# Transposing the eleventh feed-forward chunk with the DMA crossbar instead of TensorE

## The chip, the cores and the metric

The kernel runs on one core of a Trainium2 chip. The metric is the device time of one execution in microseconds (us). An execution is compared through the median of several runs.

## The reference, cut to what matters

Four decoder layers work on one sequence of 256 tokens with 1024 features. A layer is a token mixer (differential attention in layers 0 and 3, stick-breaking attention in layer 1, sliding-window attention in layer 2) and a SwiGLU feed-forward with a hidden width of 2816. Both sit between two RMS norms.

```python
x = x + rms_norm(mixer(rms_norm(x, g0)), g1)
f = (silu(h @ w_gate) * (h @ w_up)) @ w_down      # h = rms_norm(x, g2)
x = x + rms_norm(f, g3)
```

Everything is float32. All weights are read once; only the feed-forward is touched by the change.

## The kernel before, in words

**Two streams.** The 256 tokens are two streams of 128 rows (`stream(0)`, `stream(1)`, line 924). Both use every weight tile while it is in SBUF, the first stream ahead of the second.

**Units.** The weights come in units of 128 x 1024 float32 (512 KB). SP loads a unit into one of four `stage` buffers (`load_dma`, line 242), ACT makes the rounded high part `hi` and DVE the rest `lo` (`split`, line 254), both in a ring of eleven. A product of two float32 matrices is three TensorE products of rounded parts: high x high, low x high and high x low. One unit is six products of 512 columns for a stream.

**Feed-forward** (`ffn`, line 871). The hidden width is cut into eleven chunks of 256 (NCH = 11, c = 0 to 10). A chunk is projected by four units into one PSUM bank (`project`, line 496); ACT and DVE make t and then `h`, 128 rows by 256 hidden columns. For the down projection `h` has to be transposed, two blocks of 128 x 128, and split into `hTh` and `hTl`. `down(c)` (line 880) waits for the event `(name, "h", c)`, takes two units and adds twelve products to `acc`. The calls follow the list `downs` (line 214): behind chunk c from 1 to 8 comes `down(c - 1)`, behind chunk 9 none, behind chunk 10 `down(8)`, `down(9)` and `down(10)`.

**Two ways to transpose.** Chunks 0 to 9 go through `turn` (line 891): GpSimd copies `h` into two planes of 16-bit halves, SP issues one transposing DMA (both in `by_dma`, line 561), GpSimd puts the halves together again (`words`, line 569), ACT and DVE split (`split_rows`, line 576). Chunk 10 is transposed on TensorE behind `down(9)` (lines 914 to 919), into the PSUM bank `th`, and split from there.

**The order of the work.** `Emitter` (line 42) writes the instructions of both streams and of spawned tasks in one order. It keeps a time of its own that grows with the products it emits, a unit by 6 x 512 / 2.4 ns = 1.28 us and a transpose by 0.21 us. A generator yields `("d", ns)` to pause for that time, `("e", key)` to wait for an event and `("w",)` to take the next unit. Tasks that are due come first, then the first stream, but the second stream wherever it has yet to pass an edge (the end of a mixer's input projection, or of a layer) that the first has reached:

```python
behind = any(self.pos[1] < w <= self.pos[0] for w in self.edges)
order = mains[::-1] if behind else mains
```

The first stream may be at most LAG = 8 units ahead. Splits are emitted up to AHEAD = 3 units ahead of it and eleven ahead of the second, loads STAGE = 4 units ahead of the splits. Past the start of the first layer the calls `act`, `dve`, `pool` and `pe` (class `Start`, line 172) do not hold the emitted order any more: the framework then orders each engine's instructions by what its own model of the program takes to be ready, and prefers the one emitted first.

**Layer ends.** After `down(10)` a stream runs `post_norm` (line 457), pauses for 4.0 us, and with a layer to follow runs `pre_norm` (line 418): eight transposes of x into `tp_n` on TensorE, `xh_n` in eight pieces on ACT, `xl_n` on DVE. Then it pauses 0.6 us and projects the next mixer's first chunk. In layers 1 and 3 that chunk takes four units. In layer 2 it takes two, and a pause of 2.0 us follows. When the first stream is through with a layer, the second still has the last units of chunk 10 and then the units of chunks 8, 9 and 10 ahead of it.

Of the kernel before, what the change touches and what calls it, by code (L numbers as in the profile page):

```python
# [9 lines left out]
F32 = mybir.dt.float32  # L10
F32R = mybir.dt.float32r
# [8 lines left out]
P = 128  # L20
# [5 lines left out]
NCH = HIDDEN // 256  # L26
# [8 lines left out]
TMP = 8  # L35
# [123 lines left out]
def trunk_kernel(ctx, tc, x, positions, norm_gains, a_w_in, a_w_out, a_lambda, a_subln, b_w_in, b_w_out,  # L159
                 c_w_in, c_w_out, c_sinks, w_gate, w_up, w_down, out, depth=DEPTH):  # L160
# [4 lines left out]
    wk = ctx.enter_context(tc.tile_pool(name="wk", bufs=2))  # L165
# [3 lines left out]
    def bank(tag, s, shape, name):  # L169
        return ps.tile(shape, F32, tag=f"{tag}{s}", name=name, bufs=BANKS[tag])  # L170
# [43 lines left out]
    def downs(c):  # L214

        return range(c - 1, c) if 0 < c < NCH - 2 else range(NCH - 3, NCH) if c == NCH - 1 else ()
# [45 lines left out]
    em = Emitter(load_dma, split, len(units), edges)  # L262
# [123 lines left out]
    def transpose(o, i):  # L386
        pe.transpose(o, i, ident)
        em.t += P * COLUMN_NS * 4
# [81 lines left out]
    def rows_product(acc, ah, al, w, first, last):  # L470

        cols = [slice(h * 512, (h + 1) * 512) for h in range(2)]
        if last:
            for h, cs in enumerate(cols):
                mm3(acc[h], ah, al, w[0][:, cs], w[1][:, cs], first, last)
        else:
            for v in range(2):
                for h, cs in enumerate(cols):
                    mm(acc[h], ah, w[v][:, cs], first and v == 0, False)
            for h, cs in enumerate(cols):  # L480
                mm(acc[h], al, w[0][:, cs], False, False)
# [14 lines left out]
    def project(s, xn, n, units_, name, first, tag="mm"):  # L496

        b = bank("acc" if first else tag, s, [P, n], f"mm_{name}")
        per = KT // units_
        for u in range(units_):  # L500
            w = yield ("w",)
            js = [(per * u + j, slice(j * n, (j + 1) * n)) for j in range(per)]
            for kt, cs in js:
                for v in range(2):
                    mm(b, xn[0][:, kt, :], w[v][:, cs], kt == 0 and v == 0, False)
            for kt, cs in js:
                mm(b, xn[1][:, kt, :], w[0][:, cs], False, kt == KT - 1)
        return b
# [52 lines left out]
    def by_dma(src, n, name):  # L561

        planes = wk.tile([P, 2, n * P], U16, tag="t2k", name=f"hp_{name}", bufs=TMP)
        pool.tensor_copy(planes, src.bitcast(U16).rearrange("p (n w) -> p w n", w=2))
        turned = wk.tile([P, 2, n, P], U16, tag="t2k", name=f"hq_{name}", bufs=TMP)
        nc.sync.dma_start_transpose(turned.rearrange("p w b t -> p (w b) t"), planes.rearrange("p w n -> p (w n)"))
        return turned

    def words(dst, turned):

        pool.tensor_copy(dst.bitcast(U16).rearrange("p b (t w) -> p w b t", w=2), turned)
# [4 lines left out]
    def split_rows(oT, sl, src, scale=None):  # L576

        hi, lo = oT[0][:, sl, :], oT[1][:, sl, :]
        if scale is None:
            act.activation(hi, src, AF.Copy)  # L580
            dve.tensor_tensor(lo, src, hi.bitcast(F32), ALU.subtract)
        else:
            act.activation(hi, src, AF.Copy, scale=scale)
            dve.scalar_tensor_tensor(lo, src, scale, hi.bitcast(F32), ALU.mult, ALU.subtract)
# [286 lines left out]
    def ffn(s, i, xn):  # L871
        name = f"f{i}{s}"
        half = sm.tile([P, 1], F32, tag=f"half{s}", name=f"half_{name}", bufs=1)
        hsq = sm.tile([P, 1], F32, tag=f"hsq{s}", name=f"hsq_{name}", bufs=1)
        dve.tensor_scalar(half, xn[2], 0.5, None, ALU.mult)
        dve.tensor_tensor(hsq, half, xn[2], ALU.mult)
        acc = None
        hT = {}

        def down(c):  # L880
            nonlocal acc
            yield ("e", (name, "h", c))
            for j in range(2):
                w = yield ("w",)
                if acc is None:
                    acc = [bank("acc", s, [P, 512], f"acc_{name}_{q}") for q in range(2)]
                j2 = 2 * (c % 2) + j
                rows_product(acc, hT[c][0][:, j2, :], hT[c][1][:, j2, :], w, c == 0 and j == 0, c == NCH - 1 and j == 1)
            del hT[c]

        def turn(c, h):
            yield ("d", 2600)
            turned = by_dma(h, 2, f"{name}{c}")
            yield ("d", 4200)
            if c % 2 == 0:
                hT[c] = hT[c + 1] = [wk.tile([P, 4, P], F32R, tag=f"o{q}{s}", name=f"hT{q}_{name}{c}") for q in "hl"]
            t = wk.tile([P, 2, P], F32, tag="t2k", name=f"hx_{name}{c}", bufs=TMP)
            words(t, turned)
            split_rows(hT[c], slice(2 * (c % 2), 2 * (c % 2) + 2), t)
            em.set((name, "h", c))  # L900

        for c in range(NCH):
            chunk = yield from project(s, xn, 512, 4, f"{name}{c}", c == 0, ("tp", "mm")[c % 2])
            t = wk.tile([P, 256], F32, tag=f"as{s}", name=f"t_{name}{c}", bufs=STEPS)
            h = wk.tile([P, 256], F32, tag=f"as{s}", name=f"h_{name}{c}", bufs=STEPS)
            act.activation(t, chunk[:, 0:256], AF.Tanh, scale=half)
            dve.scalar_tensor_tensor(t, t, 1.0, chunk[:, 0:256], ALU.add, ALU.mult)
            dve.scalar_tensor_tensor(h, t, hsq, chunk[:, 256:512], ALU.mult, ALU.mult)
            if c < NCH - 1:
                em.spawn(turn(c, h))  # L910
            for d in downs(c):
                if d < NCH - 1:
                    yield from down(d)
        tp = bank("mm", s, [P, 2, P], f"th_{name}")
        for j in range(2):
            transpose(tp[:, j, :], h[:, j * P:(j + 1) * P])
        hT[c] = [wk.tile([P, 4, P], F32R, tag=f"o{q}{s}", name=f"hT{q}_{name}{c}") for q in "hl"]
        split_rows(hT[c], slice(2 * (c % 2), 2 * (c % 2) + 2), tp)
        em.set((name, "h", c))
        yield ("d", 700)  # L920
        yield from down(NCH - 1)
        return acc

    def stream(s):
        if s:
            yield ("d", 1500)
        for i in range(depth):
            kind = i % 3
            xn = pre_norm(s, 4 * i, f"n{i}{s}")
            yield ("d", 600)  # L930
            if i == 0 and s:
                scalars()
                act.on = dve.on = pool.on = pe.on = False
            gain = gain_of(i, 1)
            oT, name = yield from (layer_a, layer_b, layer_c)[kind](s, i, xn)
            acc = yield from out_proj(s, oT, name, (1, 1, 3)[kind])
            post_norm(s, acc, gain, f"m{i}{s}")
            yield ("d", 4000)
            gain = gain_of(i, 3)
            xn = pre_norm(s, 4 * i + 2, f"q{i}{s}")  # L940
            yield ("d", 600)
            acc = yield from ffn(s, i, xn)
            post_norm(s, acc, gain, f"e{i}{s}")
            if i < depth - 1:
                yield ("d", 4000)
        for h in range(2):
            cs = slice(h * 512, (h + 1) * 512)
            nc.sync.dma_start(out[0, s * P:(s + 1) * P, cs], xs[s][:, cs])
# [27 lines left out]
```

## Time and profile before

| what | us |
|---|---|
| median of 3 runs | 1189.04 |
| lowest and highest run | 1188.76, 1190.87 |
| the profiled execution's own time | 1188.92 |
| its span, first to last instruction | 1187.1 |

The profile is of one execution. Instructions are told by engine (PE is TensorE's products, PEld its weight loads, DVE, ACT, POOL for GpSimd, SPq for SP's DMA issues) and by the names of the tiles they write and read. A helper records most operations, so most have line 182; one goes by tiles. Times are from the start of the span. Products overlap in TensorE: a row's duration is longer than the distance to the next row, so what an operation costs is read from the starts.

### The profile page before, as it was taken

Reading aid. Unit: us, or ns where it says so; the run is one execution under the profiler, and the core shown is the slowest. Engines: PE = TensorE matmul, PEld = TensorE weight load, DVE = VectorE, ACT = ScalarE, POOL = GpSimd, SP = SyncE. Lnnn points to the kernel's source line nnn. Section 1 sums busy time; section 2 is a strip of 40 time slices with the busy share of each in tenths; the row PEclk is TensorE's granted clock in tenths of the full one; section 3 lists DMA queues with packets and bytes.
Section 4 is the critical chain, followed back from the end, with each engine's and each line's share of the span. In section 5 each row is a group of like instructions: output and inputs, shape, how many; then the busy total and the mean of one; then the engine's idle time right before and its main releaser. Section 6 shows DMA issues by size and latency. Waiting matters only on the chain.

```text
span 1187.1 us, 16727 instructions
## 1 busy us (share of the span) xinstructions
PE 1165.9 (98%) x5868; PEld 958.5 (81%) x5868; DVE 784.4 (66%) x1217; ACT 651.9 (55%) x1197; POOL 214.3 (18%) x301
## 2 busy tenths in 40 slices
PE   8999999999999999999999999999999999999997
PEld 7787788888878878888888878888878788888886
DVE  7876665665847666665688666566586785666563
ACT  6665554444756655444476655445475565545442
POOL 2000132222200013222210013221210001322221
PEclk9999999999999999999999999999999999999999
DMA  7635467776743546777764246777765454677761
GB/s 280 212 122 161 146 189 222 209 213 199 239 143 125 178 143 185 216 219 209 200 214 141 90 147 195 213 210 210 207 214 154 137 175 128 177 213 214 208 194 41
DMA packets 184360, 216.41 MB, mean 182 GB/s; under 512 B 53074, under 2 KB 148436, under 8 KB 184276
## 3 DMA queue, kind: packets, MB, share of 16 engines
q1 hardware_dynamic: 183568, 215.00, 61.1%
q8 instruction: 46, 0.75, 0.3%
q10 hardware_dynamic: 708, 0.34, 0.1%
q14 instruction: 38, 0.31, 0.1%
HBM read 203.76 MB, written 1.05 MB: 173 GB/s over the span
## 4 chain that ended last, share of the span: by engine, by line
PE 90%; DVE 3%; ACT 3%; DMA 2%; issue 2%; POOL 1%; ACTq 0%; POOLq 0%; DVEq 0%; SPq 0%
PE mm_f L182 39%; PE acc_f L182 19%; PE acc_a L182 3%; PE mm_c L182 2%; PE acc_b L182 2%; PE sc_a L182 2%; PE acc_c L182 2%; DMA stage<-in_a_w_in_dram 1%; ACT hi L182 1%; DVE lo L182 1%; PE sc_c L182 1%; PE sc_b L182 1%; PE pv_a L182 1%; DVE x L182 1%; PE tp_q L182 1%
## 5 line engine op out<-in xcount | busy, mean ns | idle before, releaser
L182 DVE TENSOR_TENSOR lo<-stage,hi 128x1024 fp32r<-128x1024 f32 x378 | 459.7, 1226 | 162.0 <-ACT hi L182 159.9
L182 ACT ACTIVATE hi<-stage 128x1024 fp32r<-128x1024 f32 x378 | 394.9, 1056 | 163.3 <-PE mm_f L182 86.9
L182 PE MATMUL mm_f<-hi,xh_q 128*128 128x512 f32 x704 | 275.7, 392 | 1.5 <-ACT hi L182 1.5
L182 PE MATMUL mm_f<-lo,xh_q 128*128 128x512 f32 x704 | 274.2, 389 | 0.0
L182 PE MATMUL mm_f<-hi,xl_q 128*128 128x512 f32 x704 | 217.2, 390 | 0.4 <-DVE xl_q L182 0.4
L182 POOL COPY hp_f<-h_f 128x512 uint16<-128x512 uint16 x80 | 90.6, 1132 | 407.7 <-DVE h_f L182 393.7
L182 PEld LDWEIGHTS mm_f<-hi,xh_q 128*128 128x128 f32 x704 | 132.1, 188 | 30.5 <-ACT hi L182 3.2
L182 PEld LDWEIGHTS mm_f<-hi,xl_q 128*128 128x128 f32 x704 | 132.2, 188 | 28.7 <-DVE xl_q L182 1.2
L182 PEld LDWEIGHTS mm_f<-lo,xh_q 128*128 128x128 f32 x704 | 132.3, 188 | 26.9
L182 ACT ACTIVATE hTh_f<-hx_f 128x256 fp32r<-128x256 f32 x80 | 33.4, 418 | 166.8 <-POOL hx_f L182 166.8
L182 PE MATMUL acc_f<-hi,hTh_f 128*128 128x512 f32 x352 | 111.5, 393 | 1.2 <-ACT hTh_f L182 1.2
L182 PE MATMUL acc_f<-hi,hTl_f 128*128 128x512 f32 x352 | 109.8, 390 | 0.0
L182 PE MATMUL acc_f<-lo,hTh_f 128*128 128x512 f32 x352 | 109.8, 390 | 0.0
L182 DVE TENSOR_TENSOR hTl_f<-hx_f,hTh_f 128x256 fp32r<-128x256 f32 x80 | 33.9, 424 | 106.0 <-ACT hTh_f L182 106.0
L182 POOL COPY hx_f<-hq_f 128x512 uint16<-128x512 uint16 x80 | 81.0, 1013 | 85.6 <-DMA hq_f<-hp_f 85.1
L182 ACT ACTIVATE t_f<-mm_f,half_f 128x256 f32<-128x256 f32 x88 | 41.5, 472 | 74.4 <-PE mm_f L182 74.4
L182 PEld LDWEIGHTS acc_f<-hi,hTh_f 128*128 128x128 f32 x352 | 65.8, 188 | 15.5 <-ACT hTh_f L182 2.3
L182 PEld LDWEIGHTS acc_f<-lo,hTh_f 128*128 128x128 f32 x352 | 66.1, 188 | 13.8
L182 PEld LDWEIGHTS acc_f<-hi,hTl_f 128*128 128x128 f32 x352 | 66.0, 188 | 13.7
L182 DVE SCALAR_TENSOR_TENSOR t_f<-t_f,mm_f 128x256 f32<-128x256 f32 x88 | 36.8, 418 | 32.5 <-ACT t_f L182 32.4
L182 DVE SCALAR_TENSOR_TENSOR h_f<-t_f,hsq_f,mm_f 128x256 f32<-128x256 f32 x88 | 42.3, 480 | 2.9
L182 ACT ACTIVATE e_a<-sc_a,nm_a 128x128 f32<-128x128 f32 (+1 forms) x64 | 26.0, 420 | 17.0 <-DVE nm_a L182 16.9
(588 smaller groups left out, 1552.3 us busy)
## 6 DMA issues: line engine op xcount, KB each, us to landing
stage<-in_ffn_w_gate_dram SPq DMA_DIRECT2D x176, 256.0 KB, 3.0
stage<-in_ffn_w_up_dram SPq DMA_DIRECT2D x176, 256.0 KB, 3.3
stage<-in_ffn_w_down_dram SPq DMA_DIRECT2D x88, 512.0 KB, 4.4
stage<-in_a_w_in_dram SPq DMA_DIRECT2D x48, 512.0 KB, 4.4
stage<-in_b_w_in_dram SPq DMA_DIRECT2D x24, 512.0 KB, 4.1
stage<-in_a_w_out_dram SPq DMA_DIRECT2D x16, 512.0 KB, 3.5
stage<-in_c_w_in_dram SPq DMA_DIRECT2D x10, 512.0 KB, 4.4
gain<-in_norm_gains_dram SPq DMA_DIRECT2D x8, 512.0 KB, 4.3
```

The lines of the kernel that those rows point to most:

```text
L182: i = call(*args, **kw)
```

## The change

Chunk 10 goes through `turn` like the others. In the last layer's second stream (`alone`) the task instead transposes on TensorE after its first pause. For chunk 10 the event is set 1.6 us (of the emitter's time) after the splits are emitted. The loop no longer treats chunk 10 apart, and the block behind it goes.

```diff
+        alone = i == depth - 1 and s == 1
...
         def turn(c, h):
-            yield ("d", 2600)
-            turned = by_dma(h, 2, f"{name}{c}")
-            yield ("d", 4200)
+            if alone and c == NCH - 1:
+                yield ("d", 2600)
+                t = bank("mm", s, [P, 2, P], f"th_{name}")
+                for j in range(2):
+                    transpose(t[:, j, :], h[:, j * P:(j + 1) * P])
+            else:
+                yield ("d", 2600)
+                turned = by_dma(h, 2, f"{name}{c}")
+                yield ("d", 4200)
+                t = wk.tile([P, 2, P], F32, tag="t2k", name=f"hx_{name}{c}", bufs=TMP)
+                words(t, turned)
             if c % 2 == 0:
                 hT[c] = hT[c + 1] = [wk.tile([P, 4, P], F32R, tag=f"o{q}{s}", name=f"hT{q}_{name}{c}") for q in "hl"]
-            t = wk.tile([P, 2, P], F32, tag="t2k", name=f"hx_{name}{c}", bufs=TMP)
-            words(t, turned)
             split_rows(hT[c], slice(2 * (c % 2), 2 * (c % 2) + 2), t)
+            if c == NCH - 1:
+                yield ("d", 1600)
             em.set((name, "h", c))
...
-            if c < NCH - 1:
-                em.spawn(turn(c, h))
+            em.spawn(turn(c, h))
             for d in downs(c):
-                if d < NCH - 1:
-                    yield from down(d)
-        tp = bank("mm", s, [P, 2, P], f"th_{name}")
-        for j in range(2):
-            transpose(tp[:, j, :], h[:, j * P:(j + 1) * P])
-        hT[c] = [wk.tile([P, 4, P], F32R, tag=f"o{q}{s}", name=f"hT{q}_{name}{c}") for q in "hl"]
-        split_rows(hT[c], slice(2 * (c % 2), 2 * (c % 2) + 2), tp)
-        em.set((name, "h", c))
-        yield ("d", 700)
-        yield from down(NCH - 1)
+                yield from down(d)
         return acc
```

## Rows read from the trace of the kernel before

**Rows 1.** The page: busy time by engine, and the chain that ended last by engine.

```profile
PE 1165.9 (98%) x5868; PEld 958.5 (81%) x5868; DVE 784.4 (66%) x1217; ACT 651.9 (55%) x1197; POOL 214.3 (18%) x301
...
PE 90%; DVE 3%; ACT 3%; DMA 2%; issue 2%; POOL 1%; ACTq 0%; POOLq 0%; DVEq 0%; SPq 0%
```

**Rows 2.** Tile th_f, whole run: durations (ns, min/median/max), and who waited (us, times).

```profile
L182 PE MATMUL th_f<-ident,h_f x16: 269/271/272, 298.4 to 1177.0; 128*128 128x128 f32 x16
...
  PE acc_f L182: 0.5, 1
```

**Rows 3.** PE in order of time, first stream, end of layer 0 (start us, us).

```profile
297.98 0.62 PE L182 MATMUL acc_f<-hi,hTl_f 128*128 128x512 f32 x2
298.44 0.38 PE L182 MATMUL th_f<-ident,h_f 128*128 128x128 f32 x2
...
298.89 0.40 PE L182 MATMUL mm_f<-lo,xh_q 128*128 128x512 f32 x1
```

**Rows 4.** All engines in order of time, second stream, end of layer 0.

```profile
309.80 0.47 DVE L182 SCALAR_TENSOR_TENSOR h_f<-t_f,hsq_f,mm_f 128x256 f32<-128x256 f32 x1
...
312.27 0.38 PE L182 MATMUL th_f<-ident,h_f 128*128 128x128 f32 x2
...
312.49 1.04 PE L182 MATMUL tp_n<-ident,x 128*128 128x128 f32 x8
312.69 0.38 ACT L182 ACTIVATE hTh_f<-th_f 128x256 fp32r<-128x256 f32 x1 [1.06 <-PE th_f L182]
...
313.28 0.71 PE L182 MATMUL acc_f<-hi,hTh_f 128*128 128x512 f32 x2
...
313.68 1.06 ACT L182 ACTIVATE hi<-stage 128x1024 fp32r<-128x1024 f32 x1 [0.61 <-DMA stage<-in_b_w_in_dram]
...
314.65 2.16 ACT L182 ACTIVATE xh_n<-tp_n,gains 128x128 fp32r<-128x128 f32 x8
```

**Rows 5.** PE in order of time, second stream, ends of layers 1 and 2.

```profile
612.46 0.63 PE L182 MATMUL acc_f<-lo,hTh_f 128*128 128x512 f32 x2
613.75 0.39 PE L182 MATMUL mm_c<-hi,xh_n 128*128 128x256 f32 x1 [0.66 <-ACT xh_n L182]
...
878.58 0.63 PE L182 MATMUL acc_f<-lo,hTh_f 128*128 128x512 f32 x2
880.10 0.50 PE L182 MATMUL mm_a300q<-hi,xh_n 128*128 128x512 f32 x1 [0.90 <-ACT xh_n L182]
```

**Rows 6.** PE in order of time, second stream, end of layer 3.

```profile
1176.91 0.38 PE L182 MATMUL th_f<-ident,h_f 128*128 128x128 f32 x2
1177.83 0.73 PE L182 MATMUL acc_f<-hi,hTh_f 128*128 128x512 f32 x2 [0.53 <-ACT hTh_f L182]
```

**Rows 7.** Tile hq_f, whole run: durations (ns, min/median/max) and landing of the DMA.

```profile
L566 SPq DMA_TRANSPOSE hq_f<-hp_f x80: 1188/1190/2057, 135.3 to 1164.1; - x80
L182 POOL COPY hx_f<-hq_f x80: 752/764/1749, 143.4 to 1170.1; 128x512 uint16<-128x512 uint16 x80
...
DMA to landing us min/median/max: 2.4/2.8/5.2
```

**Rows 8.** DVE in order of time: first and last step of one chunk, steady part, layer end.

```profile
249.28 0.48 DVE L182 SCALAR_TENSOR_TENSOR h_f<-t_f,hsq_f,mm_f 128x256 f32<-128x256 f32 x1
...
255.93 0.43 DVE L182 TENSOR_TENSOR hTl_f<-hx_f,hTh_f 128x256 fp32r<-128x256 f32 x1 [1.10 <-ACT hTh_f L182]
...
298.24 0.48 DVE L182 SCALAR_TENSOR_TENSOR h_f<-t_f,hsq_f,mm_f 128x256 f32<-128x256 f32 x1
...
308.00 0.41 DVE L182 TENSOR_TENSOR hTl_f<-hx_f,hTh_f 128x256 fp32r<-128x256 f32 x1
```

**Rows 9.** DVE and POOL in order of time: chunk 0 of layer 0, first stream.

```profile
134.04 0.48 DVE L182 SCALAR_TENSOR_TENSOR h_f<-t_f,hsq_f,mm_f 128x256 f32<-128x256 f32 x1
...
143.02 0.30 POOL L182 TENSOR_SCALAR u_m<-ssp_m 128x1 f32<-128x1 f32 x1 [7.76 <-ACT junk_m L182]
...
146.01 0.42 DVE L182 TENSOR_TENSOR hTl_f<-hx_f,hTh_f 128x256 fp32r<-128x256 f32 x1
```

## The prediction

> **What bounds the kernel now.** I read the totals and the chain first: TensorE is busy for 98% of the span and carries 90% of the chain that ended last [rows 1]. The product groups of the feed-forward are what it runs, so the reader should count everything in TensorE time: an operation taken off it is worth its spacing there, and one added to another engine costs nothing until TensorE waits for its result. Next I read the tile of the transposes that the change moves. There are eight pairs, one for each stream in each layer, and in the whole run only one product waited for their result, for 0.5 us [rows 2]. Then the instructions in order of time round three kinds of place: the first stream's end of a feed-forward [rows 3], the second stream's end with a layer to follow [rows 4, 5], and the very end [rows 6].
>
> **What goes from TensorE.** Seven of the eight pairs go. What a pair costs is read from starts, not from the 271 ns of a row: two products start at 297.98 and about 0.23 later, the pair follows at 298.44, and the second product behind it starts at 298.89 [rows 3]. Without the pair that product would be second at 298.21 + 2 x 0.23 = 298.66. So a pair costs 0.23 us, the spacing of one product. For the first stream four pairs go: 4 x 0.23 = 0.92 us. I see no stall there to win besides.
>
> **What comes in, on other engines.** Each of the seven chunks gets what the first ten have: a GpSimd copy, a crossbar DMA whose issue holds SP for 1.19 us and which lands in 2.8 us (2.4 to 5.2), a second GpSimd copy of 0.76 us, and the same two splits as before, from SBUF instead of PSUM [rows 7]. POOL's whole 214.3 us hold 80 such pairs of copies [rows 1], so at most 2.7 us for one and 19 us for seven, on an engine that is busy 18%. I cost that at nothing, and SP's 7 x 1.19 us too: by the code a load is issued four units ahead of its split and the split up to three ahead of the first stream. Without that cover a load behind the DMA would be late by its 1.19 us and its split with it. The cover of the chain itself is that chunk 10's products come late enough; the next two parts ask whether they do.
>
> **First stream.** Its chunk 10 is followed by four units of chunks 8 and 9, and a unit of the second stream stands between any two, since the lag is at its limit of 8. In the emitter's time the event comes 2.6 + 4.2 + 1.6 us after the chunk, each pause rounded up to whole units of 1.28: after nine units, where the old order also resumed (eight units, the pair, 0.7 us, one unit). So the order on TensorE stays, minus the pair. Nine units of 6 x 0.227 = 1.36 us are 12 us; the chain from the end of h to the end of the low half takes 6.6 us in the steady part (249.76 to 256.36) and 9.7 at the end of a layer (298.72 to 308.41) [rows 8]. Hidden in both: gain 0.92 us.
>
> **Second stream, three layer ends.** Here the order changes. Before, the pair, the eight transposes of the first stream's next pre-norm and then the twelve products of chunk 10 stood in this order [rows 4]; those products, 2.7 us, hid the making of xh for the next layer. After, chunk 10 cannot be emitted until its event, about 10.3 us behind the chunk in emitter time; chunks 8 and 9 use up 5.1, the pre-norm 1.7, a pause 0.6, so two or three units of the first stream's next layer come in between. They need xh at once. So one wait is taken away (TensorE waited until 613.75 and until 880.10 for xh, with chunk 10's last eight products queued behind; the first end shows none) and another put in its place:
> - Gone: the pair, 0.23 each; the stalls. The second of two products starts about 612.46 + 0.23 = 612.69, the next was due at 612.92 and came at 613.75: 0.83 us; in the same way 880.10 against 879.04 is 1.06 [rows 5]. Together 0.69 + 1.89 = 2.58 us.
> - New: the wait for xh behind its transposes. Lower bound: the first four transposes are done halfway through a run of 0.8 us, the split of the pair's result began 0.04 us after the pair's end, and an xh piece takes 0.27 [rows 4]: about 0.25 us of stall at each end. Upper bound: as in the trace, where the scheduler put a weight split ahead of xh on ACT and that split waited 0.61 us for its DMA, so that xh began only at 314.65 [rows 4]. TensorE would be free at 313.28 - 0.23 = 313.05, and with some 0.4 us from the start of xh to its first product (an estimate: one piece and the hand-over) go on at 315.05: 2.0 us. At the two other ends it would be free four products and the pair before 612.92 and 879.04, at 611.77 and 877.89: 1.98 and 2.21 us [rows 5].
> I take the lower bound, 3 x 0.25 = 0.75 us. The split got its place in a gap between the pair's split on ACT and xh. With that split gone from this place and xh ready 0.23 us earlier, xh, which is emitted first, most likely goes first. It is close to even.
> - New too: the wait for chunk 10's own result. h is done at 309.80 + 0.47 = 310.27 [rows 4]; TensorE wants its high half at 313.05 + 0.25 + 18 x 0.227 = 317.4, 7.1 us later, and the low half 0.9 us after that. The chain of 6.6 us is in time, the one of 9.7 is 1.7 late [rows 8]. At the second end only two units fit in, as the emitter pauses after the next layer's first two, so it is wanted some 1.2 us sooner. Bounds 0 and, with 1.7 + 2.9 + 1.7, some 6 us for the three; I take 0.6 in all, near the steady chain, as the scalars of the other stream's norm, behind which the copy of the longest chain stood [rows 9], are over by then.
> Behind a waiting product all of TensorE's queue waits; behind a waiting second copy only POOL's norm scalars, which need the same chunk anyway; behind the waiting DMA on SP the next layer's loads, whose units are then four to eight ahead.
>
> **The very end.** The last layer's second stream keeps its pair, but it is emitted 2.6 us after the chunk, three units on, and one unit of 1.36 us stays behind it. Now the pair starts at 1176.91 and the first product that uses it at 1177.83; without waiting it would start 0.23 after 1176.91: 0.69 us of idle TensorE [rows 6]. The path from pair to product, 0.92 us, fits under the unit: gain 0.69.
>
> **Sum:** 0.92 + 2.58 - 0.75 - 0.6 + 0.69 = 2.84 us off 1188.92 us, the profiled execution's own time (span 1187.1 and 1.8 around it): 1186.1. It stands 0.12 below the median of 1189.04, within the spread of the runs.
>
> Against this stands a rule. TensorE's pair shows 271 ns for one transpose, while the DMA's issue alone is 1.19 us and its landing 2.8 [rows 2, 7]. The Trainium skill's VectorE: DVE Perf Modes, The three transpose paths, gives 390 ns for TensorE and 1309 ns for the crossbar and, in its rules for authors, sends a 128x128 transpose to TensorE where a PSUM destination will do, as it does here. The trace agrees on the order of the two. By that rule each of the seven would lose; this is the third rival below, priced from rows.
>
> **Rivals.**
> 1. *xh behind the weight split at all three ends.* For it: the trace has just this order, with the DMA wait [rows 4], and at the two other ends TensorE waits for xh even behind four products [rows 5]. Against: the instruction that opened the gap goes. Stalls 2.0 + 1.98 + 2.21 = 6.2 instead of 0.75 + 0.6; 0.92 + 2.58 + 0.69 - 6.2 = -2.0: 1190.9 us.
> 2. *One end goes so and the others as forecast.* 2.0 - 0.25 - 0.2 = 1.55 us of the gain lost: 1187.7.
> 3. *The chain is late at the second stream's ends* (slower). Place: the second GpSimd copy and the two splits ahead of chunk 10's products. With 9.7 us the stalls are about 1.7 + 2.9 + 1.7 = 6.3: 1188.92 - 3.44 + 6.3 = 1191.8; with the 11.9 us of a layer's first chunk (134.52 to 146.43 [rows 9]) some 6.6 more, 1198. It decides from about 10 us on. For it: both long chains stand beside a norm, as here. Against: in the long one the copy stood behind POOL's scalar of the other stream's norm [rows 9], and none is due at this place.
>
> **How the numbers follow.** About 0.2% (2.4 us) is what a measurement of this kernel can tell from no change. Forecast: 0.47; its spread, 1185.5 (nothing late) to 1187.5, puts 0.33 past the bound and 0.14 inside. Rival 2: 0.15 (0.12 the same). Rival 1: 0.20, half inside, half slower. Rival 3: 0.14, slower. Left: 0.04, a larger gain. Faster 0.40, same 0.37, slower 0.23. The range is 1184.6 to 1191.8: it takes in the first two rivals and the near edge of the third, and leaves out its far part. The likeliest case's own range is 1185.5 to 1187.5.
>
> **What would show it.** Right: two transposes of this tile instead of sixteen; on TensorE at the second stream's three ends the pre-norm's transposes, under 0.5 us of idle time, two or three units of the next layer, then chunk 10 with little wait; xh ahead of the split that waits for a DMA; at the end the pair inside chunk 9 and no idle time before the last twelve products. Wrong: about 2 us of TensorE idle behind the pre-norm's transposes (rival 1), or products of chunk 10 that wait over 1 us for their high half (rival 3); a first stream that waits there would break the step I cost at nothing.

## The result and the profile after

The changed kernel is slower: 1197.18 us in the median (four runs, 1196.83 to 1197.35) against 1189.2, ratio 1.0066 [1.0055, 1.0078]. The profiled execution took 1197.2 us with a span of 1195.4, 8.3 us more between the first and the last instruction than before. The forecast was 1186.1, with a range from 1184.6 to 1191.8.

The changed kernel's page, its line of busy times:

```profile
PE 1167.5 (98%) x5854; PEld 959.8 (80%) x5854; DVE 787.2 (66%) x1217; ACT 650.9 (54%) x1197; POOL 233.8 (20%) x315
```

and its tiles th_f and hq_f over the whole run (durations in ns, min/median/max):

```profile
L182 PE MATMUL th_f<-ident,h_f x2: 270/270/271, 1184.1 to 1184.2; 128*128 128x128 f32 x2
```

```profile
L566 SPq DMA_TRANSPOSE hq_f<-hp_f x87: 1188/1190/1940, 136.2 to 1174.3; - x87
L182 POOL COPY hx_f<-hq_f x87: 750/762/2093, 144.3 to 1178.7; 128x512 uint16<-128x512 uint16 x87
```

The change does what it says: fourteen transposes fewer on TensorE, seven DMA transposes more, 19.5 us more work on POOL (the prediction bounded it at 19). Totals don't tell where 8 us went. What does is the list of what TensorE waited for (total us, times, longest). The changed kernel's first three lines are

```profile
PE mm_c L182 <- ACT xh_n L182: 2.8, 1, 2.8
PE mm_a300q L182 <- ACT xh_n L182: 2.8, 1, 2.8
PE mm_b100q L182 <- ACT xh_n L182: 2.4, 1, 2.4
```

These are the first products of layers 2, 3 and 1: the second stream's three layer ends, where before only 0.66 and 0.90 us were waited for xh [rows 5]. The transposes of the pre-norm, then the next product, in order of time on TensorE, at the first and the third end:

```profile
312.90 1.04 PE L182 MATMUL tp_n<-ident,x 128*128 128x128 f32 x8
316.34 0.79 PE L182 MATMUL mm_b100q<-hi,xh_n 128*128 128x512 f32 x1 [2.40 <-ACT xh_n L182]
316.93 0.63 PE L182 MATMUL mm_b100q<-lo,xh_n 128*128 128x512 f32 x1
317.36 0.63 PE L182 MATMUL mm_b100q<-hi,xh_n 128*128 128x512 f32 x1
...
887.89 0.50 PE L182 MATMUL mm_a300q<-hi,xh_n 128*128 128x512 f32 x1 [2.80 <-ACT xh_n L182]
888.23 0.39 PE L182 MATMUL mm_a300q<-lo,xh_n 128*128 128x512 f32 x1
888.46 0.39 PE L182 MATMUL mm_a300q<-hi,xh_n 128*128 128x512 f32 x1
```

Two things are to be seen. TensorE has nothing to do behind the transposes, for 2.4 and 2.8 us. And after the first of these waits the products come 0.43 us apart, after the third 0.23. The windows of the changed kernel around the first wait (busy us and instructions by engine, then the granted clock, the DMA share, GB/s) say why:

```profile
300.00:312.90 12.90, 12.90 (x58) 10.64 (x57) 11.97 (x16) 9.30 (x15) 5.97 (x7) 1.00 0.58 184
312.90:316.10 3.20, 1.04 (x9) 0.79 (x7) 1.85 (x3) 0.48 (x2) 1.86 (x2) 1.00 0.80 218
316.10:319.50 3.40, 3.16 (x8) 2.48 (x9) 2.79 (x10) 3.40 (x10) 0.00 (x0) 0.50 1.03 373
319.50:330.00 10.50, 10.50 (x49) 8.62 (x48) 6.91 (x8) 5.86 (x11) 1.02 (x3) 1.00 0.63 202
```

For 3.4 us TensorE ran at 0.5 of its clock, 1.2 GHz, which costs 1.7 us more. The same happened at the second end (0.50 from 619.9 to 623.3), not at the third.

What holds xh up is read on ACT, here for the three ends in turn:

```profile
310.26 2.00 ACT L182 ACTIVATE hi<-stage 128x1024 fp32r<-128x1024 f32 x2
315.62 0.42 ACT L182 ACTIVATE hTh_f<-hx_f 128x256 fp32r<-128x256 f32 x1 [3.36 <-POOL hx_f L182]
315.94 2.15 ACT L182 ACTIVATE xh_n<-tp_n,gains 128x128 fp32r<-128x128 f32 x8
...
618.15 0.42 ACT L182 ACTIVATE hTh_f<-hx_f 128x256 fp32r<-128x256 f32 x1 [3.19 <-POOL hx_f L182]
618.47 1.90 ACT L182 ACTIVATE xh_n<-tp_n,gains 128x128 fp32r<-128x128 f32 x7
...
887.17 0.42 ACT L182 ACTIVATE hTh_f<-hx_f 128x256 fp32r<-128x256 f32 x1 [3.77 <-POOL hx_f L182]
887.49 2.15 ACT L182 ACTIVATE xh_n<-tp_n,gains 128x128 fp32r<-128x128 f32 x8
```

Chunk 10's own split `hTh` stands ahead of xh. It waits for POOL's second copy, that for the DMA, and ACT does nothing for 3.2 to 3.8 us although xh's input has been there since 313.9. The Trainium skill, TensorE: Matmul & The Clock Gate, says in the table at its head that the queues of ScalarE, VectorE and GpSimd are strict FIFO. The trace agrees: xh's input was 1.7 us old when `hTh` began, and xh still came behind it.

POOL at the first end shows the chain that `hTh` waits for:

```profile
309.82 1.55 POOL L182 COPY hp_f<-h_f 128x512 uint16<-128x512 uint16 x1 [2.27 <-DVE h_f L182]
311.46 1.06 POOL L182 TENSOR_SCALAR u_n<-ss_n 128x1 f32<-128x1 f32 x1
312.61 1.40 POOL L182 TENSOR_TENSOR r_n<-u_n,mhalf 128x1 f32<-128x1 f32 x1
314.83 0.75 POOL L182 COPY hx_f<-hq_f 128x512 uint16<-128x512 uint16 x1 [0.82 <-DMA hq_f<-hp_f]
```

From 309.82 to the start of `hTh` it takes 5.8 us. By the 6.6 us that the prediction read for the whole chain in the steady part it isn't late here; it is merely waited for too early. At the two other ends it takes 6.2 us, and there the second copy itself took 2.08 and 2.09 us instead of 0.75. At the second end, POOL and then DVE:

```profile
616.04 2.08 POOL L182 COPY hx_f<-hq_f 128x512 uint16<-128x512 uint16 x1 [1.57 <-DMA hq_f<-hp_f]
...
615.15 2.35 DVE L182 TENSOR_TENSOR lo<-stage,hi 128x1024 fp32r<-128x1024 f32 x2
```

The copy began while DVE was making the low parts of two weight units and ended 0.62 us behind them. So 1.3 us of what ACT stood still at each of these two ends come from that; the last section has the rest of this.

**Where the 8.3 us lie.** I took the start of the first up-projection product of the run, of the last one in each layer, and the end, from both traces, and subtracted. The stretch from one layer's last up-projection to the next layer's holds one second-stream end and one first-stream end.

| kernel | start | layer 0 | 0 to 1 | 1 to 2 | 2 to 3 | to the end |
|---|---|---|---|---|---|---|
| after | +0.87 | -0.24 | +3.49 | +2.90 | +1.55 | -0.30 |

The 0.87 is no effect: twelve kernels with the same instructions there start 0.2 to 1.1 us later than the profile of before. The three ends make 7.9. By rows, wait less the old wait, plus 1.7 where the clock fell, less a pair of 0.23 for either stream: 2.40 + 1.7 - 0.46 = 3.6, 2.81 - 0.66 + 1.7 - 0.46 = 3.4, 2.80 - 0.90 - 0.46 = 1.4.

### The profile page after: what moved, and what is told of

It reads as the page before. It is cut to its first block, busy times and chain, and to the rows that moved or that the text cites. A ratio compares the mean times of both kernels' runs of the same rounds, so it can differ in the third digit from the quotient of the medians.

```text
span 1195.4 us, 16748 instructions
## 1 busy us (share of the span) xinstructions
PE 1167.5 (98%) x5854; PEld 959.8 (80%) x5854; DVE 787.2 (66%) x1217; ACT 650.9 (54%) x1197; POOL 233.8 (20%) x315
## 4 chain that ended last, share of the span: by engine, by line
PE 88%; DVE 3%; ACT 3%; DMA 2%; POOL 2%; issue 1%; ACTq 0%; POOLq 0%; DVEq 0%
PE mm_f L182 38%; PE acc_f L182 18%; PE acc_a L182 3%; PE mm_c L182 2%; PE acc_c L182 2%; PE acc_b L182 2%; PE sc_a L182 2%; DMA hq_f<-hp_f 1%; ACT hi L182 1%; DVE lo L182 1%; PE pv_a L182 1%; PE sc_b L182 1%; DMA stage<-in_a_w_in_dram 1%; DVE x L182 1%; POOL hx_f L182 1%
## 5 line engine op out<-in xcount | busy, mean ns | idle before, releaser
L182 POOL COPY hp_f<-h_f 128x512 uint16<-128x512 uint16 x87 | 100.7, 1157 | 400.5 <-DVE h_f L182 386.6
L182 ACT ACTIVATE hTh_f<-hx_f 128x256 fp32r<-128x256 f32 x87 | 36.3, 418 | 193.6 <-POOL hx_f L182 193.6
L182 DVE TENSOR_TENSOR hTl_f<-hx_f,hTh_f 128x256 fp32r<-128x256 f32 x87 | 36.9, 424 | 121.9 <-ACT hTh_f L182 121.9
L182 POOL COPY hx_f<-hq_f 128x512 uint16<-128x512 uint16 x87 | 89.6, 1030 | 100.6 <-DMA hq_f<-hp_f 100.2
L182 POOL TENSOR_TENSOR os_a<-os_a,mhalf 128x4 f32<-128x4 f32 x8 | 8.1, 1015 | 144.9 <-DVE os_a L182 144.9
```

What stands on the lines that cost most here:

```text
L182: i = call(*args, **kw)
```

## The experiments

Each kernel was compared in five rounds with the kernel before on the same chip (its median there 1189.46, 1189.47 and 1189.93 in the three groups of runs). The edits are against the changed kernel. Each expectation explains its own letters. The second table is the one above for all of them, less the start:

| kernel | median | ratio | interval |
|---|---|---|---|
| e1, first stream only | 1191.12 | 1.0015 | 1.0006 to 1.0024 |
| e2, second stream only | 1190.87 | 1.0010 | 1.0001 to 1.0019 |
| e3, split behind xh and xl | 1192.17 | 1.0023 | 1.0014 to 1.0032 |
| e9, split on POOL | 1195.84 | 1.0053 | 1.0039 to 1.0066 |
| e7, pre-norm earlier | 1194.72 | 1.0041 | 1.0029 to 1.0054 |
| e8, all behind | 1198.10 | 1.0073 | 1.0059 to 1.0086 |
| e10, split and copy behind | 1193.35 | 1.0029 | 1.0017 to 1.0040 |
| e4, pair early everywhere | 1189.64 | 1.0001 | 0.9992 to 1.0009 |
| e5, pair early at the very end | 1189.10 | 0.9997 | 0.9988 to 1.0006 |
| e6, pair early in layers 2, 3 | 1188.42 | 0.9992 | 0.9983 to 1.0001 |
| e11, e6 and first stream | 1187.61 | 0.9982 | 0.9974 to 0.9991 |

| kernel | layer 0 | 0 to 1 | 1 to 2 | 2 to 3 | to the end |
|---|---|---|---|---|---|
| e1 | -0.24 | -0.28 | +1.37 | -0.05 | +0.01 |
| e2 | +0.03 | +0.17 | +0.95 | +0.23 | -0.02 |
| e3 | -0.20 | +0.01 | +2.56 | +0.69 | -0.29 |
| e9 | -0.22 | +2.45 | +3.19 | +1.89 | -0.74 |
| e7 | -0.22 | +4.23 | -0.27 | +2.41 | -0.32 |
| e8 | -0.24 | +0.94 | +5.83 | +0.34 | -0.28 |
| e10 | -0.22 | +0.47 | +2.98 | +1.08 | -0.32 |
| e4 | -0.23 | +0.26 | +1.60 | -0.89 | -0.79 |
| e5 | +0.03 | +0.61 | -0.31 | -0.28 | -0.82 |
| e6 | +0.05 | +0.51 | -0.20 | -1.04 | -0.81 |
| e11 | -0.21 | +0.47 | -0.58 | -0.93 | -0.84 |

Stretches where a kernel has the instructions of before differ by up to 0.6 (e5, 0 to 1), so a single entry of that size or less says nothing by itself.

### e1 and e2: one stream each

`new` stands for the test that either kernel has in three places; where it doesn't hold, the block of before stays.

```diff
+        new = s == 0                            # e1
+        new = s == 1 and i < depth - 1          # e2
...
-            em.spawn(turn(c, h))
+            if c < NCH - 1 or new:
+                em.spawn(turn(c, h))
```

> Only the first stream's chunk 10 goes through the crossbar; the second stream keeps its pair on TensorE. Theory Q (the loss lies in ACT's queue at the second stream's three layer ends, where the split of chunk 10, waiting for its transposing DMA and second GpSimd copy, stands ahead of xh): no idle time of over 1.2 us on TensorE at the layer ends, the same stalls there as before the change, and about 0.9 us less than before, 1188.3. Rival D (the added copies and DMAs cost time wherever they are, through POOL, SP or the DMA engines): four sevenths of the loss, about 1193.

> Only the second stream's chunk 10 in layers 0 to 2 goes through the crossbar; the first stream and the very end stay as before. Theory Q: the whole loss and more, since the gains of the first stream (0.9) and of the end (0.5 to 0.7) are missing: 1189.2 + 7.9 + 1.5 = about 1198.6, with TensorE idle for 2.5 to 3 us behind the pre-norm's transposes at each of the three ends. Rival D: three sevenths of the loss, about 1192.6.

e1 took 1191.12, e2 1190.87. Both miss theory Q, by 2.8 and 7.7 us, and lie nearer to rival D's 1193 and 1192.6. But the places don't fit a price for each transpose. In the column for layer 0, where only the first stream's chunk differs, e1 gains 0.24, as do the other kernels with that chunk on the crossbar (0.20 to 0.24). e1's loss, 1.4, lies in the stretch with the second stream's middle end, which it does not touch (a product waits 0.89 us for chunk 10's low half at 614.40, and the next feed-forward's first product for xl at 695.54 0.62). e2 is the plainer miss for the theory as I had put it. It has the three DMA transposes of the second stream, and its median is only 1.4 us above before. Its ACT, at the first and the third end:

```profile
314.06 2.17 ACT L182 ACTIVATE xh_n<-tp_n,gains 128x128 fp32r<-128x128 f32 x8 [1.28 <-PE tp_n L182]
316.86 0.42 ACT L182 ACTIVATE hTh_f<-hx_f 128x256 fp32r<-128x256 f32 x1 [0.64 <-POOL hx_f L182]
...
879.92 2.17 ACT L182 ACTIVATE xh_n<-tp_n,gains 128x128 fp32r<-128x128 f32 x8 [1.28 <-PE tp_n L182]
883.21 0.42 ACT L182 ACTIVATE hTh_f<-hx_f 128x256 fp32r<-128x256 f32 x1 [1.12 <-POOL hx_f L182]
```

Here xh goes first; the clock does not fall at the ends, and no product waits for xh. So with the same transposes the large waits are gone, and what differs on ACT is the place of the split in its queue. That place is the scheduler's choice, and it differs between two kernels whose code at these ends is the same. And even with the good order the ends gain nothing: TensorE now waits for xl instead (0.91 us at the second end), as at 882.52 in

```profile
881.14 0.39 PE L182 MATMUL mm_a300q<-lo,xh_n 128*128 128x512 f32 x1
882.52 0.76 PE L182 MATMUL mm_a300q<-hi,xl_n 128*128 128x512 f32 x2 [0.99 <-DVE xl_n L182]
```

### e3: the order set by hand

The same code, but the two splits of chunk 10 are queued behind the last pieces of xh (ACT, `made["a"]`) and xl (DVE, `made["v"]`).

```diff
-            split_rows(hT[c], slice(2 * (c % 2), 2 * (c % 2) + 2), t)
+            if c == NCH - 1 and s == 1 and not alone:
+                with tc.issue_after(made["a"].ins), tc.issue_after(made["v"].ins):
+                    split_rows(hT[c], slice(2 * (c % 2), 2 * (c % 2) + 2), t)
+            else:
+                split_rows(hT[c], slice(2 * (c % 2), 2 * (c % 2) + 2), t)
```

> The changed kernel, but at the second stream's three ends the two splits of chunk 10 are queued behind the pieces of xh (on ACT) and of xl (on DVE) of the other stream's pre-norm. Nothing else moves. Theory Q: the idle time behind the pre-norm's transposes falls from 2.6 to 3.0 us to under 0.6, the clock stays at full speed, and the time falls by 7 to 10 us to 1187 to 1190. Rival L (the chain of chunk 10 itself is what TensorE waits for): the idle time moves to the products of chunk 10, 1 us or more at each end, and the time stays above 1193. Rival W (the weight split waits for its load ahead of xh): about 2 us idle at each end stay.

Measured 1192.17: 5 of the 7.7 us by which the changed kernel's median exceeds the 1189.46 come back, with one change of order and the same seven transposes. That is the strongest evidence for the queue. But 1187 to 1190 was missed; most of what is left lies from layer 1 to 2 (2.56). On TensorE the wait for xh is gone there, and a wait for xl is in its place (1.66 us at the third end):

```profile
612.95 0.28 PE L182 MATMUL mm_c<-lo,xh_n 128*128 128x256 f32 x1
614.83 1.10 PE L182 MATMUL mm_c<-hi,xl_n 128*128 128x256 f32 x3 [1.60 <-DVE xl_n L182]
```

and on DVE the pieces of xl stand behind four tables of the other stream's norm and three weight splits:

```profile
610.37 0.25 DVE L182 TENSOR_SCALAR crk_c<-cosf,r_n 128x64 f32<-128x64 f32 x1 [1.47 <-POOL r_n L182]
...
611.03 3.49 DVE L182 TENSOR_TENSOR lo<-stage,hi 128x1024 fp32r<-128x1024 f32 x3
614.43 2.15 DVE L182 SCALAR_TENSOR_TENSOR xl_n<-tp_n,gains,xh_n 128x128 fp32r<-128x128 f32 x8
```

The clock was 0.50 for 3.4 us behind this wait too. In the kernel before, chunk 10's twelve products covered the making of xl as well as that of xh.

### e9: the splits taken off ACT and DVE

```diff
-            split_rows(hT[c], slice(2 * (c % 2), 2 * (c % 2) + 2), t)
+            if s == 1 and c == NCH - 1 and not alone:
+                sl = slice(2 * (c % 2), 2 * (c % 2) + 2)
+                pool.tensor_copy(hT[c][0][:, sl, :], t)
+                pool.tensor_tensor(hT[c][1][:, sl, :], t, hT[c][0][:, sl, :].bitcast(F32), ALU.subtract)
+            else:
+                split_rows(hT[c], slice(2 * (c % 2), 2 * (c % 2) + 2), t)
```

> The changed kernel, with the two splits of chunk 10 in the second stream's three layer ends on POOL instead of ACT and VectorE; no queue order is set by hand, POOL's first copy and the crossbar transpose stay as they are. Theory D (the loss is ACT standing at its split of chunk 10 with xh queued behind, and the clock drop that follows that idle time): TensorE's wait of 2.4 to 2.8 us for xh falls under 1 us at all three ends, the granted clock does not fall there, and of the 8 us lost 5 or more come back: 1189.5 to 1192.5, near the kernel with the splits queued behind xh (ratio 1.0023). Rival W (xh is late because of the weight splits ahead of it and the norm, and the split of chunk 10 only shares the gap): the wait for xh stays over 2 us and the time at 1196 to 1198. Rival L (POOL's slower splits make chunk 10's products late): waits of over 1 us for the high half, 1193 to 1196.

Measured 1195.84, which is rival L's time. No product waits for xh any more, so W falls: what held xh was the split. That much of D came out; its gain did not, and the clock fell once (0.50 for 3.4 us behind the middle end's wait). The first line of TensorE's waits is now

```profile
PE acc_f L182 <- POOL hTh_f L182: 6.6, 3, 3.0
```

TensorE's own queue now has chunk 10's products behind four products of the next layer, and they wait for the transpose:

```profile
615.03 0.28 PE L182 MATMUL mm_c<-lo,xh_n 128*128 128x256 f32 x1
618.26 0.50 PE L182 MATMUL acc_f<-hi,hTh_f 128*128 128x512 f32 x1 [2.96 <-POOL hTh_f L182]
```

The three waits are 1.09, 2.96 and 2.52 us, so L's sign came too, though not by the slower splits that it names: POOL's two took 0.40 and 0.74 us. At the second and third end the second copy took 3.26 and 3.23. The wait moved from ACT's queue into TensorE's.

### e7: the cover given back

The first stream's pre-norm comes ahead of chunk 9's products, which then cover xh and xl, and POOL's first copy comes behind the norm's scalar (`made["p"]`).

```diff
+                late = s == 1 and c == NCH - 1
...
+                if late:
+                    with tc.issue_after(made["p"].ins):
+                        turned = by_dma(h, 2, f"{name}{c}")
...
+                if c == NCH - 1 and d == NCH - 2 and s == 1 and not alone:
+                    yield ("d", 1)
```

> The changed kernel, with two edits of order at the second stream's three layer ends: the first stream's pre-norm is emitted ahead of chunk 9's products, so that they cover the making of xh, and POOL's first copy for chunk 10 is queued behind the norm's scalar. The seven crossbar transposes stay. Theory D (the loss is made of TensorE's wait for xh behind ACT's split of chunk 10, with the clock drop behind it, and of the norm's scalars behind POOL's copy): both waits are covered, no clock drop, 1186.5 to 1189. Rival Q (the crossbar transposes themselves cost, by SP's issue and the chain's length): 1191 to 1194, with chunk 10's products waiting for their high half.

Measured 1194.72, outside both ranges. The middle end came out as theory D wants (-0.27 with everything on the crossbar, against +2.90). The other two lose more than in the changed kernel (4.23 and 2.41). ACT at the first end:

```profile
313.05 1.11 ACT L182 ACTIVATE hi<-stage 128x1024 fp32r<-128x1024 f32 x1
318.34 0.42 ACT L182 ACTIVATE hTh_f<-hx_f 128x256 fp32r<-128x256 f32 x1 [4.18 <-POOL hx_f L182]
318.89 1.06 ACT L182 ACTIVATE hi<-stage 128x1024 fp32r<-128x1024 f32 x1
321.99 1.06 ACT L182 ACTIVATE hi<-stage 128x1024 fp32r<-128x1024 f32 x1 [2.04 <-DMA stage<-in_b_w_in_dram]
322.95 0.67 ACT L182 ACTIVATE t_b100q<-mm_b100q,r_n 128x512 f32<-128x512 f32 x1
```

xh is through, but now `t_b100q`, the eviction of the next layer's first result, stands behind the split and behind a weight split whose load SP issued only after the transpose (the transpose at 313.51, seven loads from 314.81). TensorE waited 3.08 us for it, and the clock fell behind that wait. At the third end ACT's split waited only 1.19 us, but two weight splits waited 1.57 and 1.56 for loads that SP had issued behind the transpose (880.78, loads from 882.08); a weight split on DVE came late by that, the rotated result `t_a300q` behind it, and TensorE waited 2.31 us for it. The clock fell there too. That fits the part of rival Q that names SP's issue; its wait of chunk 10 for the high half is not in the trace.

### e8 and e10: POOL's copy behind the norm's scalar

Both are e3 with POOL's first copy queued behind `r_n`; e8 besides starts the transpose 2.6 us later in emitter time.

```diff
+                late = s == 1 and c == NCH - 1
+                yield ("d", 5200 if late else 2600)      # e8; e10: 2600
+                if late:
+                    with tc.issue_after(made["p"].ins):
+                        turned = by_dma(h, 2, f"{name}{c}")
```

> The kernel with chunk 10's splits queued behind the pieces of xh and xl, and besides POOL's first copy for chunk 10 queued behind the norm's scalar, with the crossbar transpose 2.6 us later. Theory D (what was left of the loss in the kernel with the splits behind xh is POOL's copy ahead of the norm's scalars, at the end of layer 1): the 2.8 us lost between the ends of layers 1 and 2 go to under 1, 1189.3 to 1190.5. Rival L (the later transpose makes chunk 10's products late instead): TensorE waits 1 to 3 us for the high half at each of the three ends, 1193 to 1198. Rival S (what is left is the scheduler's other order in layer 2, whatever POOL does): 1191.5 to 1192.5 as there.

> As the kernel with the splits queued behind xh and xl, and POOL's first copy for chunk 10 queued behind the norm's scalar, the crossbar transpose as early as in the changed kernel. Theory H (of what that kernel still lost, POOL's copy ahead of the norm's scalars is the cause at the end of layer 1, and the clock drop there follows it): TensorE's wait of 1.6 us for xl there falls to about 0.9, no clock drop, 1189.8 to 1190.8. Rival X (TensorE waits for xl because chunk 10's products no longer stand between the transposes and the next layer, whatever POOL does): the wait stays at 1.3 to 1.6 us; 1190.5 to 1192.5.

e8 took 1198.1, just past rival L's range, but no product waits for the high half at any end. At the middle end chunk 10's products stand so late that the second stream's x is late, and its pre-norm waits 3.00 us for it (5.83 in the table). In e8 the tables were held up less (0.84 us instead of 1.47), and the wait for xl was still 1.29 us:

```profile
616.30 0.90 PE L182 MATMUL mm_c<-hi,xl_n 128*128 128x256 f32 x3 [1.29 <-DVE xl_n L182]
...
627.87 1.23 PE L182 MATMUL tp_n<-ident,x 128*128 128x128 f32 x8 [3.00 <-DVE x L182]
```

So here POOL's copy explains some 0.3 of the 1.6 us; in e2, where the scheduler put it behind the scalars too, the wait was 0.91, so it may be up to 0.7. The rest is xl behind weight splits with nothing to cover it. e10 lies outside both of its ranges, with X's wait (1.61 us), and tells nothing of its own: `r_n` in the edit was that of an earlier norm, the copy still stood ahead of the scalars (609.03 against 610.67), and it is in effect a repeat of e3 (1193.35 against 1192.17).

### e4, e5, e6, e11: the new order without the DMA

In e4 the second stream keeps its pair on TensorE, but early, as the changed kernel has it in the last layer. e5 does so in the last layer alone, e6 in layers 2 and 3. In e4 the first stream goes by the crossbar, in e5 and e6 it is as before. In e5, e6 and e11 the block of before stays for the chunks that the conditions leave out.

```diff
-        alone = i == depth - 1 and s == 1
+        alone = s == 1                                  # e4
+        alone = i >= depth - 2 and s == 1               # e6, e11
+        new = alone or (s == 0 and i != 1)              # e11
```

> The second stream keeps the pair on TensorE in all layers, but in the new order: emitted 2.6 us after the chunk, between the units of chunks 8 and 9, as the change does in the last layer alone; the first stream uses the crossbar. This keeps the change's order and takes the DMA out of it. Theory Q: chunk 10's split is done before the pre-norm's transposes, its products hide the making of xh again, no stall of over 0.5 us at the three ends and at the very end, and 1185 to 1187.5. Rival O (the new order of the products costs time by itself): above 1192.

> The kernel before with one part of the change: in the last layer's second stream the pair comes 2.6 us after the chunk, with a unit of chunk 9 behind it; everything else as before, no crossbar transpose of chunk 10 at all. Theory P (the prediction's last term): 0.69 to 0.8 us less idle TensorE at the end and nothing else moves, 1188.2 to 1188.8, ratio 0.9993. Rival G (gain given back: in the two kernels whose traces show the shorter end, the stretch behind the last product was 0.5 us longer): 1189.0 to 1189.3.

> The second stream's pair stays on TensorE but is emitted 2.6 us after the chunk, with a unit of chunk 9 behind it, in layers 2 and 3 only; all else as before. Theory P (the stalls at a second stream's end are the TensorE wait for xh, and an early pair leaves chunk 10's products free to cover it): the end of layer 2 gains about 0.6 us as in the kernel with the pair early in all layers, the tail 0.8; 1187.6 to 1188.2, ratio 0.9988. Rival N (what is gained at an end is given back by the stretch behind it): 1189.0 to 1189.6, no difference.

> The kernel with the second stream's pair early on TensorE in layers 2 and 3, and besides the first stream's chunk 10 by the crossbar in layers 0, 2 and 3 (not in layer 1, where the kernel with the first stream alone showed 1.6 us lost behind the end). Theory A (the gains add: 0.6 and 0.8 from the second stream, 0.24 at each of three ends of the first): 1187.2 to 1188.2, ratio 0.9984 to 0.9990. Rival N (each change of order moves the scheduler's order behind it and gives the gain back, as at the end of layer 1): 1188.6 to 1190.

e5's trace has the 0.82 us at the end that theory P wants, and nothing of the longer stretch behind it that rival G names; its median (1189.1) lies in G's range and can't tell the gain from nothing. e6 gains at both its places in the trace (1.04 and 0.81); its median, 1188.42, lies between P's range and N's, and its interval just takes in 1. e4 gains 0.9 and 0.8 there too, so its order does not cost 3 us as rival O says, but it misses Q's 1185 to 1187.5. It loses 1.6 from layer 1 to 2, as e1 does; both show a wait for xl there that before has not, at 695.54 in e1 and at 696.04 in e4. e11 leaves layer 1 out and adds the first stream's crossbar in the others: 1187.61, ratio 0.9982 [0.9974, 0.9991], faster than both kernels and within theory A's range. TensorE in e11 has no wait left at the third end, since all of chunk 10's products stand between the transposes and xh:

```profile
877.53 1.03 PE L182 MATMUL tp_n<-ident,x 128*128 128x128 f32 x8
878.32 0.71 PE L182 MATMUL acc_f<-hi,hTh_f 128*128 128x512 f32 x2
...
880.91 0.39 PE L182 MATMUL acc_f<-hi,hTl_f 128*128 128x512 f32 x1
881.13 0.39 PE L182 MATMUL mm_a300q<-hi,xh_n 128*128 128x512 f32 x1
```

Compare 0.90 us of wait in [rows 5].

## Why the prediction was wrong, step by step

- **What goes from TensorE: right.** Layer 0 shows 0.20 to 0.24 us for a first-stream pair in every kernel without it, 0.23 was worked out; the chain is hidden in the first stream, as said.
- **The very end: right in size.** 0.69 was forecast; the start of the last product, against that of the last up-projection, came 0.81 earlier, in e5 too. In the changed kernel's profile 0.5 of it is gone again behind the last product; in e5's it is not. The pair and its product on TensorE in the changed kernel, without idle time:

```profile
1184.13 0.38 PE L182 MATMUL th_f<-ident,h_f 128*128 128x128 f32 x2
1184.26 0.70 PE L182 MATMUL acc_f<-hi,hTh_f 128*128 128x512 f32 x2
```

- **Chunk 10's own result: right where it could be seen.** 0.6 us of waits were allowed. In e2 and e3, with xh first, its products waited for it at none of the three ends, nor in the changed kernel. Rival 3 did not happen.
- **The step that failed: "xh, which is emitted first, most likely goes first."** The argument looked at one thing that might stand ahead of xh, the weight split that waited 0.61 us for its load [rows 4]. That split did go behind. But the instruction that the change had turned into a wait for a DMA, chunk 10's own split, was still ahead on ACT, as it was in the kernel before [rows 4], when it waited only for TensorE. Ahead of the sum the prediction lists who queues behind a waiting product, a waiting second copy and a waiting DMA; it leaves out who queues behind the waiting splits. The stalls taken at 0.75 us in all measured 2.40 + 2.81 + 2.80 = 8.0. The prediction itself called this choice close to even.
- **It was in the profile.** It wasn't read before the forecast. The list of what ACT waited for, in the kernel before, begins

```profile
ACT hTh_f L182 <- POOL hx_f L182: 166.8, 79, 4.5
```

  79 of the 80 chunks that go by the crossbar hold ACT still, 2.1 us on average. In the steady part only weight splits stand behind, which are emitted three units ahead, so this costs nothing, and I read such a chunk as free. At a layer's end xh stands behind it.
- **Rival 1 had the right shape with another culprit.** It put 2.0, 1.98 and 2.21 us at the three ends and gave 1190.9. With the waits as measured its sum is 0.92 + 2.58 + 0.69 - 8.0 = -3.8, 1192.7; with 3.4 for the clock, which no part of the prediction had, 1196.1. Most of the rest is the later start.
- **The lower bound left xl out.** xh alone did not need its 0.25 us an end: in e2 and e3 no product waited for it. But even with xh first, xl is late: 0.91 and 0.99 us in e2, 1.28 to 1.68 in e3, e8 and e10. Only xh was bounded. With 1 to 1.5 us of that at two ends, most of the forecast gain of 2.84 would have gone even with the order hoped for; e2, which has it, measured 1.0010.
- **POOL at nothing: too low.** A second copy was taken at 0.76 us; at the second and third end it took 2.1, which ACT and xh behind it waited out. Its first copy ahead of the norm's scalars held DVE up for 1.47 us in the changed kernel and in e3, worth 0.3 us of TensorE's time by e8 and up to 0.7 by e2. SP at nothing held at the changed kernel's ends, where no weight split waited over 0.3 us for its load; in e7 some waited 1.6 to 2.0.
- **The chances.** By their own parts, "same" is 0.36 and "slower" 0.24, not 0.37 and 0.23.

What stays open: why the scheduler put `hTh` behind xh in e2 and ahead of it in the changed kernel (no trace shows its reasons), and why e1 and e4 lose 1.4 and 1.6 us from layer 1 to 2, of which the waits named are only a part.

## What to carry to other kernels

When an instruction's input is moved from a near engine to a DMA, look first at the queue of the engine that consumes it: whatever stands behind it there waits too, and no count of busy time shows it. The list of what that engine waits for, for the same instruction elsewhere in the kernel, gives the price (here 2.1 us a time). Moving the waiting instruction moves the wait to the next queue (ACT in the changed kernel, TensorE in e9, an eviction and SP's loads in e7) unless there is work to cover the chain. The one gain, 0.2% in e11, came from keeping the cover and leaving the second stream's transpose where its answer is quick, with the crossbar where nothing waits for it.

## What the runs showed of the hardware

- **The clock after a short idle.** TensorE's granted clock fell to 0.50 for 3.4 us behind waits of 2.40 and 2.81 us in the changed kernel, 3.08 and 2.31 in e7, 2.96 in e9, 1.60 in e3 and 1.61 in e10. It stayed at 1.00 behind 2.80 in the changed kernel, 2.52 in e9, 3.00 in e8, 1.66 in e3 and 1.68 in e10. The length of the wait alone doesn't decide it; where it falls, 1.7 us are added to a wait.
- **A POOL copy beside DVE's splits.** In the changed kernel's whole run 31 of the 87 second copies began while DVE made the low part of a weight unit. Each of them ended 0.60 to 0.63 us behind that split, or behind the last of the splits that followed it without a gap; the other 56 took 0.75 to 0.77 us. Beside two splits in a row it is the 2.08 us shown above, beside three it is 3.25 in e3 and e10 and 3.26 in e9. The Trainium skill, SBUF — State Buffer, SBUF: two separate sides, says that a VectorE operation with two SBUF inputs and a GpSimd operation that reads SBUF share a pair of ports and that the later one blocks until the first has finished. The trace agrees as far as it goes: the copy stood still until the splits were done, and all of a run of them, not only the one during which it came.
